# Attention: stick breaking's sums as two single-pass products of split values, and masks on the entries' blocks only

## The chip, the cores and the metric

One core of one Trainium2 chip runs the whole program. The metric is the device time of one execution in microseconds (us). TensorE (PE in the profile, with PEld for its weight loads) multiplies, VectorE (DVE) and ScalarE (ACT) do the elementwise work, SyncE's queue (SP) issues the loads.

## The reference

Two transformer blocks in a row on one sequence of 256 tokens, width 1024, float32. The first mixes a pooling branch, a sliding-window attention (`swa`, window 128) and a block attention (`moba`, plainly causal at this length). The second has a forgetting attention (`fox`, causal, with a bias from cumulated gates), a stick-breaking attention (`sb`), a gated projection of each, and a mixture of 16 experts. Every attention has 8 heads of 64. The part that the change rewrites most:

```python
def stick_breaking_attention(q, k, v):
    z = q_t . k_s / sqrt(d)
    log_beta = jax.nn.log_sigmoid(z)
    log_one_minus = jnp.where(mask, jax.nn.log_sigmoid(-z), 0.0)        # mask: s < t
    suffix = lax.cumsum(log_one_minus, axis=3, reverse=True) - log_one_minus
    A = jnp.where(mask, jnp.exp(log_beta + suffix), 0.0)
    return jnp.einsum("bhqk,bhkd->bhqd", A.astype(v.dtype), v)
```

## The kernel before

**Numbers.** The large products are computed from split values: a float32 value x becomes h, a rounded copy in the type fp32r (written by ACT), and l = x - h, also fp32r (written by DVE). A product then takes three fp32r matmuls (l·h, h·l, h·h). Weights arrive by DMA in chunks of 1 MB in the ring and in spared slabs, and `splitter` turns each into units of h and l. Smaller products, those of the attentions among them, use plain float32 matmuls, which the profile shows as two records each.

**Order of the work.** The program is written in one pass by a planner, class `Order`: it keeps a modelled time for each engine. `run_items` goes down a list of main items (mostly six matmuls each) and, after each, fires the tasks whose time has come. Tasks are generators; each `yield` gives the word back until the modelled end of what it has issued. So the order of the instructions on every engine is fixed when the program is built, and on the chip each engine takes its instructions in that order. An item with a `need` isn't written before the tasks that it names are done, and with it every main item behind it:

```python
            tasks = [x() for x in need]
            o.until(done(tasks))
            o.advance(max([t] + [x.fin for x in tasks]))
            fn()
```

**Stick breaking.** `attention` runs for each group g of four heads a unit kt = 1 (keys 128 to 255, which only the later 128 queries see; 256 columns to a bank) and then a unit kt = 0 (keys 0 to 127, 512 columns to a bank), and for `sb` only one unit at a time (`self.live < 1`). `sb_unit` issues the scores of two banks, r = 0 and r = 1, and starts `sb_half` for each. A half runs Abs, Copy, Exp and Ln on ACT, writes sp = max(z, 0) + ln(1 + e) on DVE into a buffer of the kind `sp` (three in all), sums it over the keys with a float32 matmul against the triangle `nge` (and, for kt = 0, a second one of the sp of kt = 1 against the constant `none`), adds the sums to z on DVE and takes Exp on ACT into the slab PT. A unit ends when both halves have. The halves of kt = 1 keep their two `sp` buffers until the halves of kt = 0 have used them. When both units of a group are done, `pv` multiplies PT with the values.

**What is woven with it.** While stick breaking runs, the main items are those of the first `gate_proj` of the second block (for `fox`): in each of two halves 48 matmuls of the gates (`d<-w,H` and `d<-w,L` of 512 columns) and 24 of the projection (`d<-w,YA`). The next item is

```python
        self.item(None, mt, [lambda: tasks["yf"], lambda: tasks["ys"]])
```

where `ys` is the whole stick-breaking attention, and behind it stands the second `gate_proj` (for `sb`).

**Masks.** `scores` begins each bank with a bfloat16 matmul of the identity with a mask as wide as the bank (`w<-K` in the profile), and adds the bias (`fox` only) and the products of queries and keys.

**Buffers that the change touches.** `row_a` lies in the buffer `ra` (last read in `mid_norm`; the buffer is used again in `gather`), the kind `th` has three buffers, which the gates' tanh uses as well. `fa` begins the path of the forget gates.

Of the kernel before, what the change touches and what calls it, by code (L numbers as in the profile page):

```python
# [12 lines left out]
F32 = mybir.dt.float32  # L13
F32R = mybir.dt.float32r
BF16 = mybir.dt.bfloat16
I32 = mybir.dt.int32
AF = mybir.ActivationFunctionType
OP = mybir.AluOpType
AX = mybir.AxisListType.X

P = 128
D = 1024
# [269 lines left out]
def wait(cond):  # L292
    while not cond():
        yield 0.1


def done(tasks):
    return lambda: all(x.done for x in tasks)
# [23 lines left out]
class Body:  # L322
# [502 lines left out]

        yield from self.affine_split(xs, t, self.g1, self.x_marks[t])

    def scores(self, banks, mask, bias, lhsT, rhs):

        W = banks[0].free_size() // 2  # L830
        for sc in banks:
            self.mm(sc, self.identb, mask, True, False)
        if bias:
            for r, sc in enumerate(banks):
                self.mm(sc.rearrange("p (b k) -> p b k", b=2), *bias(r), False, False)
        for b in range(2):
            for r, sc in enumerate(banks):
                self.mm(sc[:, b * W:(b + 1) * W], lhsT(r, b), rhs(r, b), False, b == 1)

    def attn_unit(self, cfg, g, qt):  # L840

        W = P * (qt + 1)
        kind = cfg["kind"]
        head = lambda r, b: 4 * g + r + 2 * b
        banks = []
        for r in range(2):
            banks.append((yield from self.take("w")))

        def bias(r):
            f = slice(r * 64, r * 64 + 16)  # L850
            return self.pick[f, g:g + 1].to_broadcast([16, P]), self.nft[f, :, :W]

        self.scores(
            [sc[:, :2 * W] for sc in banks], self.masks["q0" if qt == 0 else ("s1" if kind == "swa" else "c1")][:, :2 * W],
            bias if kind == "fox" else None,
            lambda r, b: cfg["q"](head(r, b))[:, qt * P:(qt + 1) * P], lambda r, b: cfg["k"](head(r, b))[:, :W],
        )
        yield
        halves = [self.o.spawn(self.attn_half(cfg, g, r, qt, banks[r]), self.o.next - self.o.now) for r in range(2)]
        yield from wait(done(halves))  # L860
        self.live -= 1
# [53 lines left out]
    def sb_unit(self, cfg, g, kt):  # L915

        W = 2 * P if kt == 0 else P
        head = lambda r, b: 4 * g + r + 2 * b
        banks = []
        for r in range(2):  # L920
            banks.append((yield from self.take("w")))
        self.scores(
            [sc[:, :2 * W] for sc in banks], self.masks["k0" if kt == 0 else "k1"][:, :2 * W], None,
            lambda r, b: cfg["k"](head(r, b))[:, kt * P:(kt + 1) * P], lambda r, b: cfg["q"](head(r, b))[:, kt * P:],
        )
        yield
        halves = [self.o.spawn(self.sb_half(cfg, g, r, kt, banks[r]), self.o.next - self.o.now) for r in range(2)]
        yield from wait(done(halves))
        self.live -= 1

    def sb_half(self, cfg, g, r, kt, sc):
        W = 2 * P if kt == 0 else P
        N = 2 * W
        eb = yield from self.take("p")
        e = eb[:, :N]
        self.act(e, sc[:, :N], AF.Abs)
        zb = yield from self.take("p")
        z = zb[:, :N]
        self.act(z, sc[:, :N], AF.Copy)
        self.drop(sc)  # L940
        self.preload(SET_LOG)
        self.act(e, e, AF.Exp, scale=-1.0)
        self.act(e, e, AF.Ln, bias=1.0)
        yield
        spb = yield from self.take("sp")
        sp = spb[:, :N]
        self.v.scalar_tensor_tensor(sp, z, 0.0, e, OP.max, OP.add)
        self.drop(eb)
        if kt == 1:
            cfg["sp1", g, r] = spb  # L950
        yield
        if kt == 0:
            yield from wait(lambda: ("sp1", g, r) in cfg)
        sb = yield from self.take("w")
        su = sb[:, :N]
        self.mm(su, self.nge, sp, True, kt == 1)
        if kt == 0:
            s1 = cfg["sp1", g, r]
            self.mm(su.rearrange("p (h q) -> p h q", h=2)[:, :, P:], self.none, s1[:, :2 * P].rearrange("p (h q) -> p h q", h=2), False, True)
            yield from wait(lambda: ("used", g, r) in cfg)  # L960
            self.drop(s1)
            self.drop(spb)
        else:
            cfg["used", g, r] = True
        yield
        self.v.tensor_tensor(z, z, su, OP.add)
        self.drop(sb)
        yield
        yield from wait(done(cfg["pv"][:g]))
        pt = self.pt_of(cfg, g)  # L970
        self.act(pt[kt][:, 2 * r:2 * r + 2], z.rearrange("p (h q) -> p h q", h=2), AF.Exp)
        self.drop(zb)
# [784 lines left out]
    def build(self):  # L1757
# [165 lines left out]

        def fa():
            self.quiet = False
            ps = self.take_now("w")
            out = ps[0:8, 0:256]
            for k in range(8):
                self.mm(out, self.fah[:, k], self.xl[:, k], k == 0, False)
                self.mm(out, self.fal[:, k], self.xh[:, k], False, False)  # L1930
                self.mm(out, self.fah[:, k], self.xh[:, k], False, k == 7)
            tasks["f"] = self.after_pe(self.forget(ps))

        self.item(None, fa, n2)
        self.job_b(self.hx, self.lx, self.weights_b(w, 0), lambda i, ps: self.copy_post(four(lazy("CQ", "q2"), 0), 0.125)(i, ps), need=n2)

# [92 lines left out]
        g = self.one_hot(0)  # L2029
# [161 lines left out]
```

## Time and profile before

| | |
|---|---|
| median of 3 runs | 712.07 us (710.92 to 712.26) |
| profiled execution, its own time | 710.53 us |
| its span, first to last instruction | 708.6 us |
| TensorE busy | 683.3 us (96%) |
| VectorE busy | 398.5 us (56%) |
| ScalarE busy | 322.1 us (45%) |
| mean granted TensorE clock | 0.984 |

The profiled execution's time is 1.93 us longer than its span, and 1.54 us below the median. Busy shares are means over stages with different limits; the stages that the change touches are read by themselves below.

### The profile page before, as it was taken

The page shows a single profiled execution, that of the slowest core. Times are in us where ns is not written, and L with a number is a line of the kernel's source. Part 1 is how long each engine was busy: PE and PEld are TensorE (multiplying, and loading weights), DVE is VectorE, ACT ScalarE, POOL GpSimd, SP SyncE. Part 2 cuts the span into 40 slices and gives each one's busy share as a digit, 9 for nine tenths or more (in the row PEclk, how much of TensorE's full clock was granted, in tenths as well). Part 3 has the DMA queues.
Part 4 walks back from the last instruction along what each step waited for, and adds up shares of the span by engine and source line. Part 5 has one row for each costly group of instructions (what it writes and reads, how often), then busy time and mean ns, then how long its engine had stood idle before and what let it go on. Part 6 is the DMA issues. An engine that isn't in the chain of part 4 may idle for free.

```text
span 708.6 us, 9898 instructions
## 1 busy us (share of the span) xinstructions
PE 683.3 (96%) x3846; PEld 486.5 (69%) x3846; DVE 398.5 (56%) x756; ACT 322.1 (45%) x615; POOL 9.4 (1%) x15
## 2 busy tenths in 40 slices
PE   7999999999999998999999999989999999999993
PEld 6999889878878886899887778876333333333431
DVE  6576587796756677686967846744212211311315
ACT  6544475574444567554759744523212221121113
POOL 0000000000000000000000000000000000000000
PEclk8999999999999999999999999999999999999997
DMA  9965747546756563565773894996999999999981
GB/s 357 379 237 219 269 182 285 188 178 238 269 206 238 178 223 134 184 235 189 266 292 143 306 381 156 351 385 268 407 421 419 421 421 418 422 419 419 420 357 63
DMA packets 31668, 204.50 MB, mean 289 GB/s; under 512 B 4420, under 2 KB 4932, under 8 KB 8448
## 3 DMA queue, kind: packets, MB, share of 16 engines
q1 hardware_dynamic: 29968, 200.82, 72.7%
q0 software_dynamic: 1072, 1.83, 0.7%
q10 hardware_dynamic: 576, 1.16, 0.4%
q8 instruction: 32, 0.52, 0.3%
q14 instruction: 20, 0.16, 0.1%
HBM read 203.55 MB, written 2.10 MB: 290 GB/s over the span
## 4 chain that ended last, share of the span: by engine, by line
PE 92%; DVE 4%; ACT 1%; issue 1%; DMA 1%; DVEq 0%; ACTq 0%
PE d L436 55%; PE w L436 33%; PE w L452 4%; DVE w L275 1%; DMA X<-x 1%; ACT xs L275 0%; DVE PP L275 0%; DVE L L275 0%; DVE X L1608 0%; ACT sq L275 0%; DVE sw L275 0%; ACT PP L275 0%; DVE X L275 0%; DVE ra L1546 0%; DVE th L1636 0%
## 5 line engine op out<-in xcount | busy, mean ns | idle before, releaser
L275 DVE TENSOR_TENSOR w<-ring,w 128x1024 fp32r<-128x1024 f32 (+1 forms) x166 | 156.6, 965 | 80.4 <-ACT w L275 80.2
L275 ACT ACTIVATE w<-ring 128x1024 fp32r<-128x1024 f32 (+1 forms) x166 | 136.2, 849 | 88.3 <-PE d L436 81.9
L436 PE MATMUL d<-w,H 128*128 128x512 f32 x448 | 140.9, 396 | 0.0
L436 PE MATMUL d<-H,w 128*128 128x256 f32 x672 | 121.8, 283 | 0.0
L436 PEld LDWEIGHTS d<-H,w 128*128 128x128 f32 x672 | 104.6, 192 | 0.1
L436 PEld LDWEIGHTS d<-w,H 128*128 128x128 f32 x448 | 85.8, 191 | 18.0 <-issue 0.5
L436 PE MATMUL d<-L,w 128*128 128x256 f32 x336 | 97.0, 289 | 0.0
L436 PE MATMUL d<-w,L 128*128 128x512 f32 x224 | 93.0, 415 | 3.8 <-DVE L L275 3.8
L436 PEld LDWEIGHTS d<-L,w 128*128 128x128 f32 x336 | 64.4, 192 | 1.2 <-issue 1.0
L1636 DVE TENSOR_TENSOR th<-th,w 128x512 f32<-128x512 f32 (+1 forms) x9 | 5.7, 628 | 100.6 <-PE w L436 100.6
L436 PE MATMUL d<-w,YA 128*128 128x512 f32 x224 | 60.6, 394 | 0.0
L275 ACT ACTIVATE th<-w 128x512 f32<-128x512 f32 (+1 forms) x16 | 9.4, 584 | 107.3 <-PE w L452 53.9
L436 PEld LDWEIGHTS d<-w,L 128*128 128x128 f32 x224 | 42.9, 192 | 14.8 <-DVE L L275 5.3
L275 DVE SCALAR_TENSOR_TENSOR acc<-ring,ca,acc 128x1024 f32<-128x1024 f32 x39 | 49.9, 1281 | 1.7 <-DMA ring<-weights 1.4
L436 PEld LDWEIGHTS d<-w,YA 128*128 128x128 f32 x224 | 41.8, 188 | 9.0 <-issue 0.3
L436 PE MATMUL w<-ring,ra 128*64 128x512 f32 x128 | 47.0, 598 | 0.5 <-ACT th L275 0.5
L275 ACT ACTIVATE rg<-th 128x512 fp32r<-128x512 f32 x15 | 9.4, 629 | 52.4 <-DVE th L1663 32.5
L436 PE MATMUL w<-spl,ra 128*64 128x512 f32 x96 | 32.5, 595 | 0.0
L436 PEld LDWEIGHTS w<-ring,ra 128*64 128x64 f32 x128 | 13.5, 136 | 20.0 <-issue 19.0
L436 PE MATMUL w<-ring,th 128*64 128x512 f32 x72 | 25.3, 598 | 0.0
L275 ACT ACTIVATE PP<-w,sa 128x128 f32<-128x128 f32 (+1 forms) x48 | 19.7, 426 | 8.9 <-DVE sa L275 7.5
L436 PE MATMUL d<-w,YC 128*128 128x512 f32 x96 | 23.5, 399 | 0.0
(332 smaller groups left out, 1016.8 us busy)
## 6 DMA issues: line engine op xcount, KB each, us to landing
ring<-weights SPq DMA_DIRECT2D x109, 1024.0 KB, 6.0
spl<-weights SPq DMA_DIRECT2D x16, 1024.0 KB, 17.5
CQ<-weights SPq DMA_DIRECT2D x8, 1024.0 KB, 7.7
AB<-weights SPq DMA_DIRECT2D x6, 1024.0 KB, 13.5
K<-weights SPq DMA_DIRECT2D x6, 1024.0 KB, 13.5
PT<-weights SPq DMA_DIRECT2D x5, 1024.0 KB, 15.3
H<-weights SPq DMA_DIRECT2D x5, 1024.0 KB, 18.8
L<-weights SPq DMA_DIRECT2D x5, 1024.0 KB, 19.7
```

The lines of the kernel that those rows point to most:

```text
L275: r = fn(*args, **kw)
L436: self.nc.tensor.matmul(out, lhsT, rhs, start=start, stop=stop)
L452: self.nc.tensor.transpose(out, in_, self.ident if ident is None else ident)
L1636: nc.vector.tensor_tensor(h[:, c], gate[:, c], res[1][:, c], OP.mult)
```

## The change

Masks: banks with 128 columns to a head, and `swa`'s later queries, keep their order (mask first). For `moba` and `fox` with qt = 1 and for `sb` with kt = 0, the bank now begins with the bias or the scores, and a mask of two blocks of 128 columns (256 instead of 512) is added behind them, on the block that has entries (columns 128 to 255 of each head, or 0 to 127 for `sb`).

Sums: sp is written in place of e; ACT copies it as fp32r into an `sp` buffer (h), DVE writes l = sp - h, and the sums are two fp32r matmuls, of l and of h, against fp32r copies of the two constants, which `fa` makes in the buffer `ra`. For kt = 1 h and l share one `sp` buffer; for kt = 0 h fills one, and l goes to the rest of `ra` (r = 0) or to a `th` buffer (r = 1).

```diff
-        for sc in banks:
-            self.mm(sc, self.identb, mask, True, False)
+        if diag is None:
+            for sc in banks:
+                self.mm(sc, self.identb, mask, True, False)
...
+        if diag is not None:
+            for sc in banks:
+                self.mm(two(sc)[:, :, diag:diag + P], self.identb, mask.rearrange("p (b k) -> p b k", b=2), False, True)
...
-        spb = yield from self.take("sp")
-        sp = spb[:, :N]
-        self.v.scalar_tensor_tensor(sp, z, 0.0, e, OP.max, OP.add)
+        self.v.scalar_tensor_tensor(e, z, 0.0, e, OP.max, OP.add)
+        yield
+        hb = yield from self.take("sp")
+        lb = None
+        if kt:
+            h, l = hb[:, :N].bitcast(F32R), hb[:, N:].bitcast(F32R)
+        elif r:
+            lb = yield from self.take("th")
+            h, l = hb.bitcast(F32R), lb.bitcast(F32R)
+        else:
+            h, l = hb.bitcast(F32R), self.sums_of[:, 2 * P:2 * P + N]
+        self.act(h, e, AF.Copy)
+        yield
+        self.v.tensor_tensor(l, e, h.bitcast(F32), OP.subtract)
         self.drop(eb)
...
-        self.mm(su, self.nge, sp, True, kt == 1)
+        self.mm(su, self.sums_of[:, 0:P], l, True, False)
+        self.mm(su, self.sums_of[:, 0:P], h, False, kt == 1)
         if kt == 0:
-            s1 = cfg["sp1", g, r]
-            self.mm(su.rearrange("p (h q) -> p h q", h=2)[:, :, P:], self.none, s1[:, :2 * P].rearrange("p (h q) -> p h q", h=2), False, True)
+            s1, h1, l1 = cfg["sp1", g, r]
+            late = su.rearrange("p (h q) -> p h q", h=2)[:, :, P:]
+            for i, x in enumerate((l1, h1)):
+                self.mm(late, self.sums_of[:, P:2 * P], x.rearrange("p (h q) -> p h q", h=2), False, i == 1)
...
         def fa():
             self.quiet = False
+            self.sums_of = self.tmp("ra", 1, D).bitcast(F32R)
+            self.act(self.sums_of[:, 0:P], self.nge, AF.Copy)
+            self.act(self.sums_of[:, P:2 * P], self.none, AF.Copy)
```

## Rows read from the trace of the kernel before

**Rows 1.** The profile's page, parts 1 and 2: busy time, and DMA share in 40 slices.

```profile
PE 683.3 (96%) x3846; PEld 486.5 (69%) x3846; DVE 398.5 (56%) x756; ACT 322.1 (45%) x615; POOL 9.4 (1%) x15
...
DMA  9965747546756563565773894996999999999981
```

**Rows 2.** Busy time by stretch: us, PE, PEld, DVE, ACT, POOL, PEclk, DMA share, GB/s.

```profile
301.00:327.00 26.00, 26.00 (x222) 25.72 (x222) 18.24 (x30) 12.43 (x25) 0.00 (x0) 1.00 0.68 262
...
360.00:411.00 51.00, 51.00 (x264) 38.72 (x261) 37.66 (x49) 37.28 (x62) 0.79 (x1) 1.00 0.68 256
411.00:475.00 64.00, 62.84 (x301) 51.42 (x299) 36.10 (x49) 27.76 (x38) 0.00 (x0) 1.00 0.82 308
...
485.00:490.00 5.00, 5.00 (x38) 3.66 (x38) 1.81 (x8) 2.79 (x5) 0.00 (x0) 1.00 0.35 144
...
510.00:520.00 10.00, 10.00 (x48) 3.33 (x45) 3.34 (x8) 1.26 (x2) 1.02 (x1) 1.00 1.02 424
```

**Rows 3.** Chain that ended last, 354 to 412 us: start, us, what.

```profile
365.82 0.43 PE w L436 x2
...
372.76 2.84 PE d L436 x12
...
378.49 1.29 PE w L436 x4
```

**Rows 4.** Chain that ended last, 86 to 120 us.

```profile
102.89 2.87 PE d L436 x24
```

**Rows 5.** TensorE in order of time, 90 to 118 us: start, us, instruction.

```profile
91.96 0.39 PE L436 MATMUL w<-K 128*128 128x256 bf16 x2
92.29 0.71 PE L436 MATMUL w<-CQ 64*128 64x128 f32 x8
92.93 0.61 PE L436 MATMUL w<-K 128*128 128x512 bf16 x2
93.47 1.14 PE L436 MATMUL w<-CQ 64*128 64x256 f32 x8
```

**Rows 6.** ScalarE in order of time, 361 to 412 us.

```profile
374.94 1.29 ACT L275 ACTIVATE PP<-PP 128x512 f32<-128x512 f32 x2
...
381.03 0.61 ACT L275 ACTIVATE PT<-PP 128x512 f32<-128x512 f32 x1
...
390.54 0.42 ACT L275 ACTIVATE PT<-PP 128x256 f32<-128x256 f32 x1 [1.14 <-DVE PP L275]
...
396.14 1.30 ACT L275 ACTIVATE PP<-PP 128x512 f32<-128x512 f32 x2
397.35 1.04 ACT L275 ACTIVATE w<-ring 128x1024 fp32r<-128x1024 f32 x1
...
399.76 1.28 ACT L431 ACT_TABLE_LOAD   x1
...
403.38 0.63 ACT L275 ACTIVATE PT<-PP 128x512 f32<-128x512 f32 x1 [0.73 <-DVE PP L275]
```

**Rows 7.** VectorE in order of time, 361 to 412 us.

```profile
376.79 0.69 DVE L275 SCALAR_TENSOR_TENSOR sp<-PP 128x512 f32<-128x512 f32 x1 [0.18 <-PE w L436]
...
399.56 0.68 DVE L275 SCALAR_TENSOR_TENSOR sp<-PP 128x512 f32<-128x512 f32 x1
```

**Rows 8.** All engines in order of time, 402 to 430 us (TensorE's rows).

```profile
403.94 1.64 PE L436 MATMUL w<-PT,v 128*64 128x256 f32 x16
...
405.51 5.74 PE L436 MATMUL d<-w,YA 128*128 128x512 f32 x24
...
411.09 0.39 PE L436 MATMUL d<-w,L 128*128 128x512 f32 x1
```

**Rows 9.** Busy time by stretch, around two idle times of TensorE.

```profile
264.00:268.00 4.00, 3.21 (x19) 2.41 (x17) 4.00 (x4) 3.23 (x8) 0.00 (x0) 1.00 0.72 281
268.00:272.00 4.00, 2.95 (x8) 2.27 (x9) 3.93 (x7) 3.97 (x10) 0.00 (x0) 0.66 1.02 412
272.00:276.00 4.00, 4.00 (x17) 3.19 (x16) 3.43 (x12) 2.30 (x6) 0.00 (x0) 0.91 0.15 59
...
280.00:284.00 4.00, 2.84 (x13) 2.32 (x13) 1.38 (x3) 3.08 (x4) 0.00 (x0) 1.00 0.00 0
```

More of the change, by code (lines that the diff above doesn't have):

```diff
@@ L826, in first_norm, with scores @@
         yield from self.affine_split(xs, t, self.g1, self.x_marks[t])
-    def scores(self, banks, mask, bias, lhsT, rhs):
+    def scores(self, banks, mask, diag, bias, lhsT, rhs):
         W = banks[0].free_size() // 2
-        for sc in banks:
-            self.mm(sc, self.identb, mask, True, False)
+        two = lambda sc: sc.rearrange("p (b k) -> p b k", b=2)
+        if diag is None:
+            for sc in banks:
+                self.mm(sc, self.identb, mask, True, False)
         if bias:
             for r, sc in enumerate(banks):
-                self.mm(sc.rearrange("p (b k) -> p b k", b=2), *bias(r), False, False)
+                self.mm(two(sc), *bias(r), diag is not None, False)
         for b in range(2):
             for r, sc in enumerate(banks):
-                self.mm(sc[:, b * W:(b + 1) * W], lhsT(r, b), rhs(r, b), False, b == 1)
+                self.mm(sc[:, b * W:(b + 1) * W], lhsT(r, b), rhs(r, b), diag is not None and not bias and b == 0, diag is None and b == 1)
+        if diag is not None:
+            for sc in banks:
+                self.mm(two(sc)[:, :, diag:diag + P], self.identb, mask.rearrange("p (b k) -> p b k", b=2), False, True)
     def attn_unit(self, cfg, g, qt):
@@ L853, in attn_unit @@
         self.scores(
-            [sc[:, :2 * W] for sc in banks], self.masks["q0" if qt == 0 else ("s1" if kind == "swa" else "c1")][:, :2 * W],
+            [sc[:, :2 * W] for sc in banks], *(
+                (self.masks["s1"], None) if qt and kind == "swa" else (self.masks["q0"][:, :2 * P], P if qt else None)
+            ),
             bias if kind == "fox" else None,
@@ L922, in sb_unit @@
         self.scores(
-            [sc[:, :2 * W] for sc in banks], self.masks["k0" if kt == 0 else "k1"][:, :2 * W], None,
+            [sc[:, :2 * W] for sc in banks], self.masks["k1"][:, :2 * P], 0 if kt == 0 else None, None,
             lambda r, b: cfg["k"](head(r, b))[:, kt * P:(kt + 1) * P], lambda r, b: cfg["q"](head(r, b))[:, kt * P:],
@@ L944, in sb_half @@
         yield
-        spb = yield from self.take("sp")
-        sp = spb[:, :N]
-        self.v.scalar_tensor_tensor(sp, z, 0.0, e, OP.max, OP.add)
+        self.v.scalar_tensor_tensor(e, z, 0.0, e, OP.max, OP.add)
[12 more added lines that the diff above has]
+        self.v.tensor_tensor(l, e, h.bitcast(F32), OP.subtract)
         self.drop(eb)
         if kt == 1:
-            cfg["sp1", g, r] = spb
+            cfg["sp1", g, r] = hb, h, l
         yield
@@ L955, in sb_half @@
         su = sb[:, :N]
-        self.mm(su, self.nge, sp, True, kt == 1)
+        self.mm(su, self.sums_of[:, 0:P], l, True, False)
+        self.mm(su, self.sums_of[:, 0:P], h, False, kt == 1)
         if kt == 0:
-            s1 = cfg["sp1", g, r]
-            self.mm(su.rearrange("p (h q) -> p h q", h=2)[:, :, P:], self.none, s1[:, :2 * P].rearrange("p (h q) -> p h q", h=2), False, True)
+            s1, h1, l1 = cfg["sp1", g, r]
+            late = su.rearrange("p (h q) -> p h q", h=2)[:, :, P:]
+            for i, x in enumerate((l1, h1)):
+                self.mm(late, self.sums_of[:, P:2 * P], x.rearrange("p (h q) -> p h q", h=2), False, i == 1)
             yield from wait(lambda: ("used", g, r) in cfg)
             self.drop(s1)
-            self.drop(spb)
+            self.drop(hb)
+            if lb is not None:
+                self.drop(lb)
         else:
```

## The prediction, made before the changed kernel was run

> **What bounds the kernel now.** I read the page first: TensorE is busy 96% of the span, VectorE 56% and ScalarE 45%, and the DMA slices stand at 9 from the middle of the expert stage on [rows 1]. Then the stretches. While stick breaking runs (360 to 411 us) TensorE is busy all 51 us, VectorE 37.66 and ScalarE 37.28; from 411 to 475 TensorE is busy 62.84 of 64 [rows 2]. So up to 475 us the end moves with TensorE. In the expert stage DMA is full (1.02), but in 485 to 490 it stands at 0.35 because every buffer is taken; what restarts it is TensorE's progress [rows 2]. I therefore count a shift of TensorE before 475 us one to one at the end, in both directions.
>
> The third view is the timeline of the stick-breaking stretch, where two strands share TensorE. One is filler: the gates and projection of the first `gate_proj`. The other is a serial chain of four units, from the first scores to the first matmul of the last `pv` at 403.94. Behind that `pv` stand 24 filler matmuls (405.51, 5.74 us), and only then the next `gate_proj`, at 411.09 [rows 8]. That next `gate_proj` may not be written before stick breaking is done. So the chain has room before 411.09, and the room is what the prediction turns on.
>
> **The change part by part.**
>
> *Masks.* Two mask matmuls of 256 columns take 92.29 - 91.96 = 0.33 us up to the next instruction, two of 512 take 93.47 - 92.93 = 0.54 [rows 5]. Six units (two each of `moba`, `fox`, `sb`) get the narrow ones: 6 x 0.21 = 1.26 us less TensorE time, of which 0.84 lies ahead of stick breaking and 0.42 in it. Standing behind the scores costs nothing on TensorE, which takes them in order either way.
>
> *Sums on TensorE.* A half of kt = 0 takes 1.29 us now, one of kt = 1 0.43 [rows 3]. The new passes are of the form that the main matmuls have: 12 of 512 columns in 2.84 us, 0.237 each [rows 3], 24 of 256 columns in 2.87, 0.12 each [rows 4]. So kt = 0 becomes 2 x 0.237 + 2 x 0.12 = 0.71 and kt = 1 0.24; four pairs save 4 x (1.72 - 0.95) = 3.08 us. Bounds: with the 0.27 and 0.165 of the bfloat16 masks for a pass [rows 5] the saving is 4 x (1.72 - 2 x 0.27 - 4 x 0.165) = 2.1; nothing is saved if the passes run at the float32 rate (a rival below). I take 3.08, since form and size are those of the main matmuls.
>
> The Trainium skill (TensorE: Matmul & The Clock Gate, "Back-to-back issue gap") gives about 131 ns for each 512-column matmul in a sustained stream with weight loads; this trace has 0.237 us [rows 3]. By the page the eight passes of 512 columns would take 0.85 us less, an estimate; the measured row decides.
>
> *Sums on the other engines.* Each half gains an ACT copy and a DVE subtraction. From the nearest rows of the same width: 0.63 and 0.69 for kt = 0, 0.42 and 0.42 for kt = 1 [rows 6, 7]. Four pairs: 4.2 us ACT, 4.4 us DVE. As load this is covered (both engines idle some 13 us in the stretch [rows 2]). As latency it stands in the chain.
>
> *The chain, kt = 0.* ACT runs the four operations of r = 0 and then at once those of r = 1, so h of r = 0 now waits until r = 1 is through. And r = 1 needs an `sp` buffer which is free only when the sums of r = 0 are done: at 376.79 and 399.56 its sp starts just then, although ScalarE had finished at 376.23 and 397.44 [rows 6, 7]. That wait now takes r = 1's copy. From ScalarE's end to the last Exp's end the tail takes 381.64 - 376.23 = 5.41 us in the first group and 404.01 - 397.44 = 6.57 in the second [rows 6]. Afterwards the tail is h 0.63, l 0.69, sums 0.71, h 0.63, l 0.69, sums 0.71, addition 0.69, Exp 0.63: 5.38 us of work with seven handoffs. A handoff: from r = 1's sp the tails take 4.85 and 4.45 us for 3.3 us of work (0.69, 1.29, 0.69, 0.63) in three handoffs, 0.45 each on average. Sum 5.38 + 7 x 0.45 = 8.5; longer by 3.1 and 1.9.
>
> *The chain, kt = 1.* No buffer is missing there, r = 1 sets the end: + 0.42 + 0.42 - 0.19 (sums) + 2 x 0.45 = 1.55 each.
>
> Together the chain grows by 3.1 + 1.9 + 2 x 1.55 = 8.1 us. Low bound, with handoffs of 0.1: tails of 6.1, so +0.7 and -0.5, and 0.85 for each kt = 1: 1.9 us. High bound: a table load (1.28) and a weight copy (1.04) of the queue [rows 6] in each kt = 0 tail as well: 8.1 + 4.6 = 12.7.
>
> *The room.* TensorE's work ahead of 411.09 without the last `pv` (405.51 - 403.94 = 1.57) and less 3.08 + 0.42 ends at 411.09 - 1.57 - 3.50 = 406.0. The last `pv` can start at 403.94 + 8.1 = 412.0. So TensorE runs out of filler and waits, in pieces, some 6 us. The next `gate_proj` starts at 412.0 + 1.57 = 413.6 instead of 411.1: +2.5. With the 0.84 saved earlier: +1.7.
>
> *The clock.* After TensorE stood idle around 268 us (0.79 and 1.05 us of two neighbouring stretches) the granted clock was 0.66 in the next 4 us and 0.91 in the 4 after: 4 x 0.34 + 4 x 0.09 = 1.7 us lost, a part of the time at the lower of its two levels, 1.2 GHz; after 1.16 us idle in 280 to 284 it stayed at 1.00 [rows 9]. Waits of several us lie on the first side, but short sums in between, and part of the lost time falls into the waits: I take 1.0, bounds 0 and 1.7.
>
> *At nothing.* The two 128-column copies in `fa` cost under 0.42 each on ScalarE, which is busy 12.43 of 26 us there [rows 2]; without that cover 0.8. The `th` buffer: no row shows a wait for one; the tanh of the gates holds two of three, so I take 0; if all were held, r = 1 would wait for one projection half at most (5.74 [rows 8]). No DMA is added; the slabs that stick breaking gives back come 8 us later, into a stretch at 0.82 [rows 2], which I take as cover.
>
> *Sum.* +1.7 + 1.0 = +2.7 us. On the profiled execution 710.53 + 2.7 = 713.2 (its span 708.6 + 2.7 = 711.3); it lies 1.54 below the median, so against the median 712.07 + 2.7 = 714.7, which I predict.
>
> **The rivals.**
>
> *The chain still fits (faster).* It decides from growth below 2.1 us, where the last `pv` would be ready at 406.0. For it: the low bound is 1.9, and the present tails hold waits for TensorE behind filler. Against it: the six handoffs that each group gains cannot all be short while VectorE is busy 37.66 of 51 us. Price: -3.50 - 0.84 = -4.3, so 707.7; growth up to 5 gives down to -1.4.
>
> *The stall eats the saving and no more (same).* Growth near 6.5: 403.94 + 6.5 + 1.57 = 412.0, which is 0.9 late and balanced by 0.84. It needs a clock that stays up: 712.1.
>
> *The clock falls for longer.* The waits sit between short sums, and `pv` and the gates behind it would run at the lower level. The price from the rows: 1.7 instead of 1.0 after one fall, 3.4 after two: 715.4 to 717.1. The Trainium skill (TensorE: Matmul & The Clock Gate, "HAM oscillation — how this bites in real kernels") says that bursts of matmuls with waits between them pay the fall to half rate again and again; [rows 9] shows one fall.
>
> *The single passes are none.* If fp32r ran at the float32 rate here, 3.08 us would be missing: 717.8. The main matmuls at 0.237 speak against it.
>
> **How the numbers follow.** A measurement of this kernel tells 0.2%, 1.4 us, from no change. Forecast (stall larger than the saving, growth 7 to 10): 0.40, with its own range 712.8 to 717. Clock falls for longer: 0.16. Growth above 10 (up to 12.7: 403.94 + 12.7 + 1.57 - 411.09 - 0.84 + 1.7 = +8.0, 720): 0.04. No single passes: 0.02. Same: 0.18. Fits: 0.20. A part of the forecast (up to +1.4) counts as same, so faster 0.20, same 0.22, slower 0.58. The range leaves out half of the fits (0.10) and the top (0.06): 709.5 to 718.5.
>
> **What would show it.** Sums of a half as four TensorE records within 0.75 us; eight more ACT and eight more DVE operations in the stretch; the last `pv` behind the 24 filler matmuls instead of ahead of them, with TensorE idle before it and PEclk below 1 there; the next `gate_proj` near 413; DMA's low stretch near 488 longer by as much. Wrong, if TensorE shows no idle time between 400 and 415.

## The result, and the profile of the changed kernel

The changed kernel takes 721.68 us (median of 4 runs, 720.42 to 722.33) against 712.12 us for the kernel before on the same chip: a ratio of 1.0141 [1.0125, 1.0158], 9.6 us slower. That is the forecast direction, but three and a half times the forecast loss, and above the range's upper end of 718.5. The profiled execution takes 722.11 us with a span of 720.3 and a mean granted clock of 0.979.

The page's busy line and clock line for the changed kernel:

```profile
PE 680.2 (94%) x3846; PEld 485.3 (67%) x3846; DVE 402.5 (56%) x764; ACT 328.4 (46%) x627; POOL 9.4 (1%) x15
...
PEclk9999999999999999999999889998999999999997
```

TensorE has less work than before (680.2 us against 683.3 [rows 1]), VectorE has eight operations more, and the clock line has two dips, in the 23rd and 24th slice (about 396 to 432 us) and in the 28th (about 486 to 504 us). The windows after, with the columns of [rows 2], show where TensorE lost its time:

```profile
360.00:411.00 51.00, 42.52 (x231) 34.09 (x229) 41.03 (x56) 39.49 (x66) 0.79 (x1) 0.96 0.66 252
...
404.00:408.00 4.00, 0.00 (x0) 0.00 (x0) 3.41 (x4) 3.94 (x7) 0.59 (x1) 0.91 0.53 195
408.00:412.00 4.00, 1.06 (x3) 0.86 (x4) 1.43 (x3) 2.05 (x4) 0.20 (x1) 0.50 0.80 331
412.00:416.00 4.00, 2.62 (x8) 1.75 (x7) 1.63 (x3) 1.26 (x2) 0.00 (x0) 0.50 0.00 0
416.00:420.00 4.00, 3.61 (x17) 2.03 (x16) 0.35 (x1) 0.71 (x2) 0.00 (x0) 0.50 0.00 0
420.00:424.00 4.00, 4.00 (x12) 2.46 (x13) 0.69 (x1) 1.35 (x3) 0.00 (x0) 0.88 0.75 264
```

From 360 to 411 us TensorE was busy all 51 us before [rows 2]; now it is busy 42.52. Between 404 and 408 it does nothing at all, and from 408 to 420 it is granted the lower of its two levels (0.50, 1.2 GHz). TensorE in order of time (start, us, instruction, in brackets the idle time and what ended it) names what it waits for:

```profile
402.07 0.39 PE L436 MATMUL w<-K 128*128 128x256 bf16 x2
410.94 0.80 PE L436 MATMUL w<-ra 128*128 128x512 f32 x1 [8.48 <-DVE ra L275]
...
413.98 0.80 PE L436 MATMUL w<-th,ra 128*128 128x512 f32 x1 [1.39 <-DVE th L275]
...
415.56 1.12 PE L436 MATMUL w<-PT,v 128*64 128x256 f32 x2
417.07 2.82 PE L436 MATMUL w<-PT,v 128*64 128x256 f32 x14 [0.39 <-ACT PT L275]
...
420.90 0.82 PE L436 MATMUL d<-w,L 128*128 128x512 f32 x1
```

The masks behind the last unit's scores end at 402.46. The next work in TensorE's order is the sum of that unit's first half, whose l (in `ra`) VectorE delivers 8.48 us later. `pv`, whose first two records need only the first half's Exp and stand at 415.56, goes on at 417.07 (it began at 403.94 before) and the next `gate_proj` starts at 420.90 (411.09 before [rows 8]): 9.81 us late. The pieces: `pv` is 13.13 later; from there to the gates it takes 3.83 us instead of 1.57, since the clock is at half and two other matmuls stand in between (`w<-acc,ones` at 419.82; +2.26); and the 24 filler matmuls that stood behind `pv` are already done (405.51 to 411.09, -5.58). 13.13 + 2.26 - 5.58 = 9.81. That covers the growth of the medians, 9.6.

**The chain, unit by unit.** A unit is read from its first Abs on ScalarE to the next unit's first Abs, the last one to the time given above for `pv`. ScalarE's rows before and after:

```profile
362.86 0.66 ACT L275 ACTIVATE PP<-w 128x256 f32<-128x256 f32 x2 [1.86 <-PE w L436]
371.81 1.09 ACT L275 ACTIVATE PP<-w 128x512 f32<-128x512 f32 x2 [2.76 <-PE w L436]
382.08 0.66 ACT L275 ACTIVATE PP<-w 128x256 f32<-128x256 f32 x2 [0.44 <-PE w L436]
393.01 1.09 ACT L275 ACTIVATE PP<-w 128x512 f32<-128x512 f32 x2 [0.45 <-PE w L436]
```

```profile
361.22 0.66 ACT L275 ACTIVATE PP<-w 128x256 f32<-128x256 f32 x2 [1.86 <-PE w L436]
371.40 1.09 ACT L275 ACTIVATE PP<-w 128x512 f32<-128x512 f32 x2 [0.62 <-PE w L436]
392.15 0.66 ACT L275 ACTIVATE PP<-w 128x256 f32<-128x256 f32 x2
403.74 1.06 ACT L275 ACTIVATE PP<-w 128x512 f32<-128x512 f32 x2
```

| unit | before, us | after, us | growth | forecast |
|---|---|---|---|---|
| kt = 1, first group | 8.95 | 10.18 | +1.2 | +1.55 |
| kt = 0, first group | 10.27 | 20.75 | +10.5 | +3.1 |
| kt = 1, second group | 10.93 | 11.59 | +0.7 | +1.55 |
| kt = 0, second group | 10.93 | 13.33 | +2.4 | +1.9 |
| sum | 41.08 | 55.85 | +14.8 | +8.1 |

The chain starts 1.64 us earlier (first Abs at 361.22 instead of 362.86), so `pv` comes 14.8 - 1.64 = 13.1 later. Nearly the whole miss is in one unit. ScalarE's queue in that unit (its last row belongs to the last unit), then VectorE's:

```profile
374.53 1.30 ACT L275 ACTIVATE PP<-PP 128x512 f32<-128x512 f32 x2
375.85 1.28 ACT L431 ACT_TABLE_LOAD   x1
377.15 1.09 ACT L275 ACTIVATE th<-d 128x512 f32<-128x512 f32 x2
378.12 0.63 ACT L275 ACTIVATE sp<-PP 128x512 fp32r<-128x512 f32 x1
378.64 2.96 ACT L275 ACTIVATE w<-ring 128x1024 fp32r<-128x1024 f32 x3
382.15 0.63 ACT L275 ACTIVATE sp<-PP 128x512 fp32r<-128x512 f32 x1 [0.56 <-PE w L436]
...
389.98 1.06 ACT L275 ACTIVATE w<-ring 128x1024 fp32r<-128x1024 f32 x1 [2.43 <-PE d L436]
390.95 0.61 ACT L275 ACTIVATE PT<-PP 128x512 f32<-128x512 f32 x1
...
408.27 1.29 ACT L275 ACTIVATE PP<-PP 128x512 f32<-128x512 f32 x2
```

```profile
378.38 1.28 DVE L275 SCALAR_TENSOR_TENSOR acc<-ring,ca,acc 128x1024 f32<-128x1024 f32 x1
379.58 0.68 DVE L275 TENSOR_TENSOR ra<-PP,sp 128x512 fp32r<-128x512 f32 x1
...
380.94 3.49 DVE L275 TENSOR_TENSOR w<-ring,w 128x1024 fp32r<-128x1024 f32 x3
384.35 0.68 DVE L275 TENSOR_TENSOR PP<-PP,w 128x512 f32<-128x512 f32 x1
384.94 0.69 DVE L275 TENSOR_TENSOR th<-PP,sp 128x512 fp32r<-128x512 f32 x1
...
389.01 0.69 DVE L275 TENSOR_TENSOR PP<-PP,w 128x512 f32<-128x512 f32 x1
```

And from the chain that ended last (start, us, what) the sums of that unit's two halves, and of the last unit a half's sums and the last Exp:

```profile
381.66 0.69 PE w L436 x4
...
387.81 0.69 PE w L436 x4
...
410.94 1.66 PE w L436 x4
...
416.38 0.64 ACT PT L275
```

Follow it. ScalarE ends both halves' four operations at 375.83, as fast as before (4.43 us after the first Abs; before 4.42). The copy h of r = 0 (`sp<-PP`, 378.12) stands behind a table load and two tanh of the gates. Its l (`ra`) waits for an accumulation and starts at 379.58. Its sums wait for filler, until 381.66. Only when these are done is an `sp` buffer free for r = 1's copy (382.15). Its l (`th`, 384.94) stands behind three weight splits and r = 0's addition, its sums behind filler until 387.81, and its Exp (390.95) behind a weight copy. From 375.83 to that Exp's end at 391.56 are 15.7 us, of which the prediction's 5.38 us are work. The tail of the last unit runs from 409.56, where ScalarE ends the Exp and Ln of r = 1 that start at 408.27, to 417.02: 7.5 us, 0.9 more than before (6.57), and two of its pieces are sums at half clock (1.66 each). There the filler is used up and nothing stands in the queues between. The rest of that unit's growth lies ahead of the tail: its four operations take 5.82 us instead of 4.43, since a table load (404.82, 1.28 us) now falls among them.

### The profile page after: what moved, and what is told of

The parts are those of the page before. It is cut to its first block, busy times and chain, and to the rows that moved or that the text cites. A ratio compares the mean times of both kernels' runs of the same rounds, so it can differ in the third digit from the quotient of the medians.

```text
span 720.3 us, 9919 instructions
## 1 busy us (share of the span) xinstructions
PE 680.2 (94%) x3846; PEld 485.3 (67%) x3846; DVE 402.5 (56%) x764; ACT 328.4 (46%) x627; POOL 9.4 (1%) x15
## 4 chain that ended last, share of the span: by engine, by line
PE 68%; DMA 20%; DVE 6%; ACT 3%; issue 1%; SPq 0%; DVEq 0%; ACTq 0%
PE d L436 50%; PE w L436 16%; DMA L<-weights 6%; DMA spl<-weights 6%; DMA YA<-weights 5%; DMA ring<-weights 3%; PE w L452 2%; DVE w L275 2%; ACT PP L275 1%; DVE PP L275 1%; DMA X<-x 1%; ACT L431 1%; DVE L L275 1%; ACT xs L275 0%; DVE X L275 0%
## 5 line engine op out<-in xcount | busy, mean ns | idle before, releaser
L275 DVE TENSOR_TENSOR w<-ring,w 128x1024 fp32r<-128x1024 f32 (+1 forms) x168 | 158.9, 968 | 83.1 <-ACT w L275 82.8
L275 ACT ACTIVATE w<-ring 128x1024 fp32r<-128x1024 f32 (+1 forms) x168 | 138.1, 851 | 92.1 <-PE d L436 85.7
L436 PE MATMUL d<-w,H 128*128 128x512 f32 x448 | 138.7, 391 | 0.8 <-DVE w L275 0.8
L436 PEld LDWEIGHTS d<-w,H 128*128 128x128 f32 x448 | 84.1, 188 | 18.7 <-DVE w L275 1.6
L436 PE MATMUL d<-w,L 128*128 128x512 f32 x224 | 90.9, 406 | 6.0 <-DVE L L275 6.0
L275 DVE SCALAR_TENSOR_TENSOR acc<-ring,ca,acc 128x1024 f32<-128x1024 f32 x41 | 52.5, 1281 | 0.9 <-DMA ring<-weights 0.7
L436 PE MATMUL w<-ring,ra 128*64 128x512 f32 x136 | 36.4, 597 | 0.5 <-ACT th L275 0.5
L436 PEld LDWEIGHTS w<-ring,ra 128*64 128x64 f32 x136 | 10.7, 137 | 20.3 <-issue 19.0
L436 PE MATMUL d<-w,CV 128*128 128x512 f32 x64 | 23.2, 403 | 0.0
## 6 DMA issues: line engine op xcount, KB each, us to landing
K<-weights SPq DMA_DIRECT2D x5, 1024.0 KB, 15.7
```

Of the source, the lines that this page charges most:

```text
L275: r = fn(*args, **kw)
L436: self.nc.tensor.matmul(out, lhsT, rhs, start=start, stop=stop)
```

## The experiments

Ratios are against the kernel before in the same session (710.79 us for e1 to e4, 711.74 for e5 to e8, 711.05 for e9 to e12). Chain lengths and unit lengths are read as in the table.

**e1_masks_only.** The sums of before, the masks of the change; the part of the diff that is taken back:

```diff
-        self.act(h, e, AF.Copy)
-        self.v.tensor_tensor(l, e, h.bitcast(F32), OP.subtract)
...
+        self.mm(su, self.nge, sp, True, kt == 1)
```

> The changed kernel with the sums of before (float32 matmuls, no split): only the masks are changed. Theory (the loss is the stick-breaking chain's growth, the masks only shorten TensorE): 712.1 - 1.3 = 710.8 us, the last pv still ahead of the 24 projection matmuls. Rival (masks behind the scores lengthen the chains, or the new order of the queues costs by itself): 712 us or more.

Measured: 709.73 us, 0.9978 [0.9965, 0.9990], 1.6 us faster. In its chain the last `pv` still stands ahead of projection work:

```profile
405.67 1.45 PE w L436 x16
407.12 4.98 PE d L436 x21
```

The masks are a small gain, not a cost. The chain of this run is 44.6 us, 3.5 longer than before though no operation was added to it, and `pv` starts 1.7 later (405.60); both fit in the room, of which 6 projection matmuls are left.

**e2_sums_only.** The masks of before, the sums of the change:

```diff
-        if diag is None:
-            for sc in banks:
-                self.mm(sc, self.identb, mask, True, False)
+        for sc in banks:
+            self.mm(sc, self.identb, mask, True, False)
...
```

> The changed kernel with the masks of before: only the sums are changed. Theory: the whole loss is here, 721.7 + 1 = 722 to 723 us, with TensorE idle some 8 us before the last sums. Rival (the masks bear a part of the loss): clearly under 721 us.

Measured: 722.43 us, 1.0159 [1.0135, 1.0184]. The sums carry the whole loss, and the growth of the chain too: it is 55.2 us, 14.1 longer than before.

**e3_warm_fill.** Adds 38 matmuls of ones by ones (128 columns), whose product is thrown away, as a main item ahead of the waiting one:

```diff
+        self.item(None, lambda: self.warm(38))
         self.item(None, mt, [lambda: tasks["yf"], lambda: tasks["ys"]])
```

> The changed kernel with 38 matmuls of ones (128 columns, results unused) on TensorE ahead of the item that waits for stick breaking, about 8 us that fill its idle time. Theory that the lowered clock after the idle time is part of the loss (7.3 us of TensorE work at 0.50 between 408 and 420 us and 4 at 0.88 behind it lose about 4 us): 717.5 to 718.5 us, PEclk 1.00 there. Rival (the idle time alone is the loss, the clock's fall lies inside waits): 721 to 722 us.

Measured: 726.05 us, 1.0211 [1.0187, 1.0236], foreseen by neither. Its chain shows why:

```profile
400.97 8.48 PE d L436 x76
```

The planner wrote the 38 matmuls (76 records) ahead of the last unit's scores, which they delayed by 8.5 us. The run says nothing about the clock; e8 repeats it with a better place.

**e4_gates_first.** Moves the waiting item `mt` behind the first-half gates of the next `gate_proj`, so that TensorE has these 48 matmuls to do meanwhile. The argument `between` is called in `gate_proj` behind them:

```diff
...
+            if between and not half:
+                between()
...
-        self.item(None, mt, [lambda: tasks["yf"], lambda: tasks["ys"]])
-        self.gate_proj(w, 4104, "w_branch_sb_2", merged2, False, lambda: tasks["ys"], lambda: S["ys"], done_half=self.merged_t(merged2), gated=lambda: self.spare(["H", "L"]))
+        self.gate_proj(w, 4104, "w_branch_sb_2", merged2, False, lambda: tasks["ys"], lambda: S["ys"], done_half=self.merged_t(merged2), gated=lambda: self.spare(["H", "L"]), between=lambda: self.item(None, mt, [lambda: tasks["yf"], lambda: tasks["ys"]]))
```

> The changed kernel with the item that waits for stick breaking moved behind the gates of the first half of the next gate_proj, so that 48 more matmuls (11 us) stand ahead of it. Theory (TensorE only ran out of filler): the stall goes, 708 to 710 us, below the kernel before. Rival (ScalarE and VectorE are loaded so much that the weight splits come late, or the order is worse in general): 716 us or more.

Measured: 709.89 us, 0.9982 [0.9966, 0.9999]. The loss is gone, though the chain is even longer here (59.2 us): what cost the time was TensorE without work, not the longer chain as such. Some idle time is left (1.81 us of one stretch):

```profile
412.00:416.00 4.00, 2.19 (x10) 1.36 (x8) 2.30 (x4) 3.97 (x7) 0.00 (x0) 1.00 0.42 165
```

DMA is nearly as idle here as in the changed kernel, where its share is 0.00 from 412 to 420 (here 0.42 and 0.00), and `pv` goes on later still (420.21), so the later return of the slabs isn't what cost the time either.

**e5_before_gates_first.** The kernel before with the same move (the diff of e4).

> The kernel before with only the waiting item moved behind the gates of the first half of the next gate_proj, as in e4. Theory (the kernel before had room: its last pv stood ahead of 24 projection matmuls): no gain from more filler, 710 to 712 us. Rival (the move of the item is itself worth what e4 won back): clearly faster, 707 us or less.

Measured: 710.99 us, 0.9999 [0.9985, 1.0014]. The move is worth nothing where the chain has room, so e4 did not win by something else.

**e6_h_on_dve.** VectorE makes h, directly ahead of l:

```diff
-        self.act(h, e, AF.Copy)
-        yield
+        self.v.tensor_copy(h, e)
```

> The changed kernel with h written by VectorE right ahead of l (a copy and a subtraction in a row) instead of by ScalarE. Theory (the growth is handoffs into busy queues; in the first kt = 0 unit h waits 2.3 us behind a table load and two tanh on ScalarE): the chain is some 5 us shorter, 714 to 717 us. Rival (the growth comes from VectorE's queue, or from the sp buffer): no gain, 720 to 723 us.

Measured: 718.09 us, 1.0095 [1.0077, 1.0113], between the two expectations; chain 52.8 us, 3.0 shorter; second unit 16.65. VectorE's row:

```profile
379.11 0.42 DVE L275 CAST sp<-PP 128x512 fp32r<-128x512 f32 x1
```

l follows at 379.57. Two crossings between engines and one stand in ScalarE's queue are gone, for 0.42 us more on VectorE. It is a part of the growth, not most of it.

**e7_hold_splits.** The weight splitter waits while a half of stick breaking is between its Ln and its last Exp:

```diff
                 if self.relaxed(u):
+                    yield from wait(lambda: not self.hot)
...
         self.act(e, e, AF.Ln, bias=1.0)
+        self.hot += 1
...
         self.drop(zb)
+        self.hot -= 1
```

> The changed kernel with the splitter held back, for units that are not needed next, while a half of stick breaking stands between its Ln and its last Exp. Theory (the new operations wait behind weight splits of 1.0 to 1.2 us each, three in a row on both engines in the first kt = 0 unit): the chain is 4 to 8 us shorter, 713 to 717 us. Rival (the splits are not what it waits for): 720 us or more; a third way is that the splits held back are late for TensorE, seen as waits of the gates' matmuls.

Measured: 716.61 us, 1.0062 [1.0045, 1.0078]; chain 53.7; second unit 16.17, 4.6 shorter, but the last one 15.21, 1.9 longer. The time is as expected; the chain, 2.2 us shorter, misses the expected 4 to 8. (Its profiled execution took 718.71, the longest of the nine.) TensorE's waits from 360 to 420 us (what it waited for: us in total, times, longest) show what was traded:

```profile
PE w L437 <- DVE ra L275: 3.1, 1, 3.1
...
PE d L437 <- DVE w L275: 0.8, 1, 0.8
PE d L437 <- ACT w L275: 0.5, 1, 0.5
```

The stall of 8.5 us is 3.1, and TensorE's filler now waits for splits instead (0.8 and 0.5). The splits were a good part of the second unit's delay, and they can't simply be put off: they feed the filler.

**e8_warm_behind_scores.** The 38 matmuls of e3 as a task begun right behind the last unit's scores:

```diff
...
+        if g and kt == 0:
+            self.o.spawn(self.keep_warm(38))
         halves = [self.o.spawn(self.sb_half(cfg, g, r, kt, banks[r]), self.o.next - self.o.now) for r in range(2)]
```

> The changed kernel with 38 matmuls of ones (128 columns, unused results, some 8 us) behind the scores of the last unit, where TensorE is idle for 8.5 us; the scores themselves stay where they are. Theory that the lowered clock behind the idle time is a part of the loss: 717.5 to 719 us and PEclk near 1.00 up to the last pv. Rival (it lies inside waits): 721 us or more.

Measured: 719.53 us, 1.0114 [1.0089, 1.0138], between the two expectations. Its windows against those of the changed kernel:

```profile
404.00:408.00 4.00, 4.00 (x38) 4.00 (x38) 3.41 (x4) 3.94 (x7) 0.62 (x1) 1.00 0.58 195
...
412.00:416.00 4.00, 1.87 (x11) 1.19 (x13) 1.90 (x3) 1.57 (x3) 0.00 (x0) 1.00 0.01 4
```

With idle time replaced by useless work the clock stays at 1.00, a half's sums take 0.99 us instead of 1.66, and the next gates start at 417.68 instead of 420.90, 3.2 us earlier. In the time it is 0.0027 x 712 = 1.9 us, with intervals that overlap slightly, so the times alone don't tell it from nothing. Of its four executions the one profiled and one more show a mean clock of 0.989, the other two 0.981 and 0.980, about that of the changed kernel's profile (0.979); whether the filling matmuls kept the clock up in those was not seen. As far as these runs tell, the clock's share is some 1.9 to 3.2 us, the small part of the loss.

**e9_no_buffer_wait.** For kt = 0 and r = 1, h and l go into the slab CQ, which is given back to the loads only when stick breaking ends; r = 1 then needs neither an `sp` nor a `th` buffer:

```diff
...
-            lb = yield from self.take("th")
-            h, l = hb.bitcast(F32R), lb.bitcast(F32R)
+            h, l = self.scratch[:, 0:N], self.scratch[:, N:2 * N]
...
```

> The changed kernel with h and l of r = 1 (kt = 0) in a slab of their own (CQ, given back to the loads after stick breaking instead of before it), so that r = 1 needs no sp buffer of r = 0. Theory of the prediction (the buffer makes r = 1 wait for the sums of r = 0, about 2.5 us in each kt = 0 unit): 715 to 718 us. Rival (the wait for the buffer hides behind the other queues): 720 us or more; a further cost can come from one load buffer less for 45 us.

Measured: 713.92 us, 1.0031 [1.0017, 1.0045], faster than expected; chain 49.4, 6.5 shorter; the second unit 14.01 instead of 20.75, the last one hardly shorter (13.25 instead of 13.33), next gates at 413.27. ScalarE's rows:

```profile
378.37 0.63 ACT L275 ACTIVATE sp<-PP 128x512 fp32r<-128x512 f32 x1
378.89 0.63 ACT L275 ACTIVATE scratch<-PP 128x512 fp32r<-128x512 f32 x1
```

The second copy starts 0.52 us behind the first instead of 4.03, and so it and its l are ahead of the weight copies and splits that they stood behind. Of the three ways to shorten the chain (e6, e7, e9) this brings most. The slab also holds one load less in this stretch, an effect that the run does not separate.

**e10_gates_first_dve** joins e4 and e6 (their diffs).

> e4 (the waiting item behind 48 gate matmuls) with h on VectorE as in e6. Theory (once the chain is covered, all that is left is TensorE's saving of about 4.3 us; e4 still had 1.8 us of idle time and a lowered clock): 707 to 709 us. Rival (the saving is lost elsewhere, as TensorE isn't what the rest waits for): 710 us or more.

Measured: 707.32 us, 0.9948 [0.9928, 0.9967].

**e11_gates_first_masks** joins e1 and e4.

> e1 (only the masks changed) with the waiting item behind the gates. Theory (no stall there, so nothing to win by more filler): as e1, 709.5 to 711 us. Rival (the sums' saving can be had only with the split): no difference to e10.

Measured: 709.76 us, 0.9979 [0.9967, 0.9991], as e1 alone: with the sums of before the move has nothing to win.

**e12_gates_first_dve_no_wait** joins e4, e6 and e9.

> e10 with the slab of e9 as well: the shortest chain and the most filler. Theory: no idle time of TensorE between 400 and 420 us, 707 to 708.5 us, the best version. Rival (the load buffer that is missing for 45 us, or a new order of the queues, costs more than it brings): slower than e10.

Measured: 706.79 us, 0.9940 [0.9920, 0.9960], 4.3 us faster than before and the fastest version, though its interval overlaps that of e10. A window of it and TensorE's only wait between 360 and 430 us:

```profile
412.00:416.00 4.00, 3.62 (x16) 2.38 (x14) 4.00 (x5) 3.61 (x5) 0.00 (x0) 1.00 0.95 367
```

```profile
PE w L436 <- ACT PT L275: 0.8, 1, 0.8
```

TensorE has work while the chain runs, the clock stays up, and the saving arrives. Against e11, which has masks and move but the sums of before, the single passes with e6 and e9 are worth about 3 us (706.79 against 709.76; with e6 alone, in e10, 2.4), where the prediction had 3.08.

## Why the prediction was wrong in its size

**Right: the mechanism.** The prediction turned on the room of the chain, said that TensorE would run out of filler, that the last `pv` would come behind the 24 projection matmuls and that the next `gate_proj` would be late by what is left. All of it is in the rows, and e4 with e5 shows it: filler put into the gap takes the loss away and does nothing for the kernel before.

**Right: the sums on TensorE.** A half of kt = 0 takes 0.69 us where the clock is 1.00 (forecast 0.71). The rival without single passes is out.

**Undersized: the masks.** The prediction had 0.84 us ahead of stick breaking; the chain starts 1.64 earlier, in e1 1.84 (first Abs at 361.02). The twenty records around 92 us in the chain that ended last, before and now:

```profile
92.12 2.48 PE w L436 x20
```

```profile
92.04 2.07 PE w L436 x20
```

So one unit saves 0.41 instead of 0.21, and four of them are 1.64. It is no chance of one execution: in every kept trace with the masks of before the first Abs lies at 362.65 or later, in every one with the new masks at 361.74 or earlier. Only the mask's own share had been counted; the other half lies with the scores, whose sixteen records are now one group of 1.58 us. Why they are shorter was not tested.

**Failed: the growth of the chain, 8.1 us, with its high bound of 12.7.** It measured 14.8. The step that failed is the handoff price of 0.45 us, taken from the tails of before and put in seven times for every kt = 0 tail, and with it the time that h stands behind a table load and two tanh on ScalarE, which the sum had at nothing. In the second unit the waits are 15.7 - 5.38 = some 10.4 us. In the order of the tail: 2.3 us for ScalarE (h), 0.8 for VectorE (l), 1.4 for TensorE (sums), none for r = 1's copy once the buffer is free, 2.2 for VectorE, 2.2 for TensorE, 0.5 for VectorE (addition), 1.3 for ScalarE (Exp). So the seven handoffs cost some 8 us, 1.2 on average instead of 0.45, and h's place in ScalarE's queue 2.3 more. In the last unit, where the filler was gone, the same tail took 7.5 us, of which 5.38 is work and 2 x (1.66 - 0.69) = 1.9 the longer sums: some 0.1 us for all its waits together. In these rows a handoff has next to no price of its own; it costs what stands in the queue of the next engine, and while filler lasts weight splits, accumulations and the gates' tanh stand there. The prediction's high bound allowed for one table load and one weight copy; the unit met these, two tanh, an accumulation, three splits and the filler ahead of both sums.

The terms close. The growth is 6.7 us above the forecast, the way from `pv` to the gates 2.3 us longer where the clock's 1.0 was forecast, and the masks gave 0.8 more: 6.7 + 1.3 - 0.8 = 7.2 us. The time missed the forecast by 9.6 - 2.7 = 6.9.

The prediction did name the buffer wait, and costed it as work with handoffs in series. That hid its real price: the copy comes 3.5 us late, and its l then falls behind a batch of splits. e9 puts that at 6.5 us of chain, e6 the copy's place at 3.0, e7 the splits at 2.2. The three are not independent and don't add to the 14.8. With the waiting item moved, none of them is needed to lose the loss (e4), and with h on VectorE as well the saving of the sums arrives (e10); e7 and e9 were not tried alone with the move.

**Followed from it: the room.** Out of filler was forecast for 406.0 and came at 402.46. Of these 3.5 us 1.6 are the masks' gain (0.84 of it foreseen, but counted apart), and 1.4 are the last unit's two sums, which the prediction counted as work ahead though they stand behind the wait; 0.5 were not traced. The idle time fell into one piece of 8.5 us.

**Undersized: the clock.** Forecast +1.0 with a bound of 1.7; measured 1.9 to 3.2 (e8). The rival of the longer fall was right in kind, though it expected repeated falls and there was one long one: 0.50 for 12 us. The Trainium skill (TensorE: Matmul & The Clock Gate, "HAM oscillation — how this bites in real kernels") says that short bursts between waits keep paying the fall; the trace shows the sums and `pv` between 410 and 420 us at 0.50 (at 1.00 in e8), but one fall only. The price of 1.7 us was read from [rows 9], where 0.66 belongs to a stretch that itself has 1.05 us of idle time. That fall is not in every execution: the changed kernel, with 1.81, 0.96 and 0.41 us idle in the same three stretches, keeps 1.00 there. Nor did it cost 1.7 us further on: e5, the same as the kernel before up to there, has no such fall, idles 1.06, 0.98 and 1.17 us there instead, and its first Abs comes only 0.2 us earlier (362.65). So that fall lay for the most part in waits.

**Open.** In the profiled executions the span grows by 11.7 us, 1.9 more than the gates' delay of 9.8. A second stretch shows a difference (windows after; the clock is the number behind POOL's):

```profile
485.00:490.00 5.00, 4.58 (x23) 4.58 (x24) 4.02 (x29) 3.12 (x3) 0.00 (x0) 0.58 1.02 425
490.00:495.00 5.00, 5.00 (x35) 5.00 (x35) 1.38 (x7) 0.79 (x4) 0.00 (x0) 0.74 1.02 429
```

Around the routing the clock is 0.58 and 0.74, where the kernel before had 0.75 (475 to 480) and 0.91 (480 to 485). The mean from 470 to 500 us is 0.89 after and 0.94 before. But it is 0.89 in the profiles of e1 and e5 too, which lost nothing, so this is not shown to come from the change. The medians differ by 9.6 only, which the gates' delay covers. DMA's low stretch, forecast to be longer, came 10 us later and deeper (0.22 and 0.25 from 495 to 505, where the kernel before had 0.35 and 0.45 from 485 to 495), over the same length; what that costs was not separated.

## What to carry to other kernels

Where a serial chain is woven into filler work, price an added operation on it by the work that stands in its engine's queue at that moment, not by handoffs measured elsewhere, and follow each buffer that the operation must wait for: lateness puts it behind the next batch. Compare the chain's growth with the filler left, and before making the chain shorter look for independent work to put behind it: here moving one item brought back 11 us, and each of three ways to shorten the chain brought 3 to 8. A saving on the bound engine is real only while that engine still has work to take.

## What the runs showed of the hardware that was not expected

- The fall of the clock outlasted the idle time: 8.48 us without work were followed by the lower level up to 420 us, while sums and `pv` ran.
- The same stretch of the program shows a fall of the clock in one execution and none in another: from 268 to 276 us the profile before has 0.66 and 0.91, those of e5 and of the changed kernel 1.00, though TensorE idled more in them.
- Rounding 128x512 values to fp32r takes 0.42 us on VectorE (CAST, e6) and 0.63 on ScalarE (Copy).
